# A later planned landing for the up stage's weight loads, the parts of T ahead of the first two GLU tiles, and two products of the down stage accumulated in banks that already hold a product

## The chip, the cores and the metric

One core of one Trainium2 chip runs the whole program. The metric is the device time of one execution in microseconds (us). The engines are TensorE (PE, with its weight loads as PEld), VectorE (DVE), ScalarE (ACT), GpSimd (POOL) and SyncE (SP); SP and POOL issue the transfers here.

## The reference

One decoder layer over 512 tokens with 1024 features, all in float32. The first half (projection, retention, sparse attention, output projection, norm) is not touched by the change. The second half is

```
def conv_ffn(x, w_up, conv_w, w_down):
    u = x @ w_up                                  # 512x1024 @ 1024x5632
    u = causal depthwise convolution of width 3 over the tokens
    gate, val = split(u, 2)
    return (gelu(gate) * val) @ w_down            # 512x2816 @ 2816x1024

h = rms_norm(x, norm_ffn_pre)
x = x + rms_norm(conv_ffn(h, ...), norm_ffn_post)
```

## The kernel before

Every float32 product is made of three fast products of a rounded high part and a low remainder (high by high, high by low, low by high), so each operand has to be split: ACT copies the high part, DVE subtracts it for the low part.

**The planner.** The code does not emit instructions as it goes. Every call on an engine is recorded as an operation, with a rank: a stage number and, within a stage, its place in the program. At the end `schedule` (L262) runs through the operations with a cost for each, and at each step gives an engine the operation that can start first; among those within 20 ns of it, the one of the lowest rank. Transfers get a modelled landing (L366 to L369): one transfer after the other at 350 bytes per ns (175 for accumulating ones), and then 2000 ns for SP and 4000 ns for POOL. What comes out is a fixed order of instructions for each engine; on the chip each engine works through its own list and waits where the next instruction's operands aren't there. The costs only shape this order. Two engines that touch the same PSUM bank are ordered one after the other even where both only read (L209, L214).

**The up stage** (L1247 to L1376) makes 22 pairs of tiles of gate and value, 128 columns each. The first two pairs are plain products, `up` (L1223), into four PSUM banks `ab` of the pool `acc`, which has four. Pairs 2 to 21 are made by a Strassen scheme (`strassen`, L1293): seven products of 12 matmuls each, P1, P2, P6, P5, P7, P3, P4 in this order, P1, P6, P7, P4 in a bank `X` of the pool `m` (three banks) and P2, P5, P3 in a bank `G` of `acc`. ACT copies interim sums out of the banks (`u` twice, `p5`) before the next product may add to them. The moving operands are the hidden states and sums of their quarters, the parts of T: `MV["5"]`, `MV["6"]`, `MV["7"]` and one more for `MV["4"]`, split at L1343 to L1351. For each pair `loads` (L1266) issues three transfers on SP (`a11`, `s1`, `a12`) and four on POOL, of which three add onto what an earlier transfer or a negated copy by ACT left there (`s1`, `s3`, `w["4"]`); `prep` (L1282) makes the six split weight tiles with ACT and DVE. `loads` of the next pair is recorded before `strassen` of this one. `glu` (L1238) takes a finished pair through convolution, gelu and product; `act_sums` (L1251) adds three sums for each two pairs. The order recorded around the change is: the plain products, `glu(0)`, `glu(1)`, the parts of T, `loads(2)`, `prep(2)`, `loads(3)`, Strassen pair 2 and its `glu`, and so on.

**The down stage** (L1431 to L1530) is also a Strassen scheme. P1, P5, P6, P7 are accumulated over all 11 pairs into eight banks `DA`; sums of them go to SBUF as `base` (L1444 to L1452). Then P4, P2, P3 run in banks of their own (`E`, L1454); `norm` (L1456) adds each finished product to its `base`, squares and sums on ACT, takes the root on POOL (`rsqrt`, a power), multiplies by the norm's weights (`wfin`), scales, adds the residual and sends it out. `norm(0)` and `norm(1)` are the last work of the program; the last three pairs of P2 and P3 are made bank by bank (`end`, L1522), so that the norms can follow.

Of the kernel before, what the change touches and what calls it, by code (L numbers as in the profile page):

```python
# [12 lines left out]
ALU = mybir.AluOpType  # L13
# [117 lines left out]
PE, ACT, DVE, POOL, SP = "tensor", "scalar", "vector", "gpsimd", "sync"  # L131
# [9 lines left out]


class _Op:
    __slots__ = ("idx", "alts", "rank", "deps", "nwait", "users", "news", "tiles", "start", "end", "eng", "ready", "gelu", "floor", "load", "port")


class _Plan:


    def __init__(self, nc):  # L150
        self.nc, self.ops, self.slots, self.hist, self.order_of = nc, [], {}, {}, {}
        self.rank, self.floor = 0, None

    def engine(self, *names):
        plan = self
# [30 lines left out]
    def add(self, alts):  # L186
        op = _Op()
        method, a, k = next(iter(alts.values()))
        op.idx, op.rank = len(self.ops), (self.rank, len(self.ops))
        op.alts = {n: (*x, self.cost(n, *x)) for n, x in alts.items()}  # L190
        op.load = 0.0
        op.port = {n: self.shared(n, *x) for n, x in alts.items()}
        if PE in alts:
            op.load = size(a[1]) / (2.4 if method == "transpose" else 1.2)
        op.gelu = next((x for x in list(a) + list(k.values()) if x in (AF.Gelu_apprx_tanh, AF.Exp, AF.Tanh)), None)
        op.deps, op.users, op.news, op.tiles = {}, [], [], set()
        acc = [(x, i == 0 or n in OUTS) for i, (n, x) in enumerate([(str(i), x) for i, x in enumerate(a)] + list(k.items()))
               if isinstance(x, bass.AP)]
        for ap, w in acc:
            name = ap.tensor.name  # L200
            if name not in self.slots:
                continue
            op.tiles.add(name)
            if name not in self.hist:
                self.hist[name] = []
                op.news.append(name)
                self.order_of[name] = len(self.order_of)
            pm, fm = self.region(ap)
            psum = "PSUM" in str(ap.space)  # L209
            keep = []  # L210
            for e in self.hist[name]:
                j, w2, pm2, fm2 = e
                hit = pm & pm2 and fm & fm2
                if hit and j != op.idx and (w or w2 or psum and self.ops[j].alts.keys() != alts.keys()):  # L214
                    op.deps[j] = op.deps.get(j, False) or (w2 and not w)
                if not (w and hit and not (pm2 & ~pm) and not (fm2 & ~fm)):
                    keep.append(e)
            keep.append((op.idx, w, pm, fm))
            self.hist[name] = keep
        op.floor = self.floor if any(x[0] == "dma_start" for x in alts.values()) else None  # L220
        self.ops.append(op)
        return op
# [39 lines left out]
    def schedule(self):  # L262
# [52 lines left out]
        while len(order) < len(ops):  # L315
# [50 lines left out]
            if method == "dma_start":  # L366
                nbytes = a[0].size() * 4 if callable(a[0].size) else a[0].size * 4
                dma = max(dma, op.end) + nbytes / (175.0 if "accum_op" in k else 350.0)
                op.end = dma + (2000 if e == SP else 4000)  # L369
            for x in op.alts:  # L370
                avail[x].remove(op)
            for t in op.tiles - live:
# [30 lines left out]
def _body(ctx, tc, io, out, soff, coff):  # L403
# [50 lines left out]
    def mps(n="m"):  # L454
        return plan.tile(pp, [P, 512], F32, nm(n), "m", 3)
# [124 lines left out]
                          C("ks").unsqueeze(1).to_broadcast([P, 4, RH]), op=ALU.mult)  # L580


    def mm3(o, ah, al, bh, bl, start, stop):
        pe.matmul(o, ah, bh, start=start, stop=False)
        pe.matmul(o, ah, bl, start=False, stop=False)
        pe.matmul(o, al, bh, start=False, stop=stop)

    class Chunk:
        def __init__(self, src, lh, ll, ncols, evac, first=0):
# [648 lines left out]
    def glu(i, ag, av):  # L1238
        g = conv(ag, i)
        act.activation(g, g, AF.Gelu_apprx_tanh)  # L1240
        v = conv(av, NF + i)
        (dve_pool if i >= PL else dve).tensor_tensor(acts[i // 2][:, i % 2, :], g, v, op=ALU.mult)
        if i % 2:
            act_sums(i // 2)
# [21 lines left out]
    def loads(i):  # L1266
        g, v = io["wup"][i, 0], io["wup"][i, 1]
        a, s13 = blk(gp, "av", 4, F32), blk(st, "raw", 2, F32)
        w = {"4": blk(gp, "av", 4)}
        a11, a12, s1, s3 = a[:, 0], a[:, 1], s13[:, 0], s13[:, 1]  # L1270
        sync.dma_start(a11, g[:, 0:4])
        sync.dma_start(s1, v[:, 0:4])
        sync.dma_start(a12, g[:, 4:8])
        pool.dma_start(s1, v[:, 4:8], accum_op=ALU.add)
        copy(s3, a11, scale=-1.0)
        pool.dma_start(s3, v[:, 0:4], accum_op=ALU.add)
        pool.dma_start(w["4"][:, 1], v[:, 4:8])
        copy(w["4"][:, 0], f(w["4"][:, 1]), scale=-1.0)
        pool.dma_start(w["4"][:, 0], v[:, 4:8], accum_op=ALU.add)
        return a11, a12, s1, s3, w  # L1280

    def prep(a11, a12, s1, s3, w):  # L1282
        s24 = blk(st, "wl", 4, F32)
        b2, b4 = s24[:, 0], s24[:, 1]
        dve.tensor_tensor(b2, s1, a11, op=ALU.subtract)
        for n, src, tag in (("1", a11, "wh"), ("2", a12, "wh"), ("6", b2, "wh"), ("5", s1, "wh"), ("7", s3, "wl"), ("3", b4, "wl")):
            if n == "6":
                dve.tensor_tensor(b4, a12, b2, op=ALU.subtract)
            w[n] = blk(st, tag, 4)
            part(w[n], src)  # L1290
        return w
# [34 lines left out]
    for c0 in (0, 256):  # L1326
        for i in range(4):
            up(ab[i], ws[i], c0, c0 + 256)
    glu(0, ab[0], ab[1])
    glu(1, ab[2], ab[3])  # L1330
    MV = {n: (h2h[q][:, :, c:c + HT], h2l[q][:, :, c:c + HT]) for n, q, c in (("1", 0, 0), ("2", 1, 0), ("3", 1, HT))}
    for a in range(2):
        k = slice(2 * a, 2 * a + 2)
# [7 lines left out]
    MV["7"] = None, t3l  # L1341
    MV["4"] = h2h[0][:, :, HT:], h2l[0][:, :, HT:]
    for n, src in (("5", [t13[0]]), ("6", hb[0]), ("7", [t13[1]]), ("4", hb[1])):  # L1343
        if n == "7":
            MV[n] = vv([P, 4, HT], F32R, "T"), t3l
        h, l = MV[n]
        w = 4 // len(src)
        for a, x in enumerate(src):
            k = slice(a * w, a * w + w)
            copy(h[:, k], x)  # L1350
            dve.tensor_tensor(l[:, k], x, f(h[:, k]), op=ALU.subtract)  # L1351
# [12 lines left out]
    def v_parts(j):  # L1364
        v = part2(pt, [P, 2, HT], "a")
        split(sm_s[j], *v)
        return v

    nxt = loads(PL)
    for i in range(PL, NF):  # L1370
        now = prep(*nxt)
        if i + 1 < NF:
            nxt = loads(i + 1)
        else:
            uv = u_parts(0), v_parts(0)
        glu(i, *strassen(i, now))  # L1376
# [23 lines left out]
    def wtile(n):  # L1400
        return tuple(plan.tile(st, [P, 2, 512], F32R, nm(m), m, 4) for m in ("wh", "wl"))

    def product(o, a, b, tt, start, stop):
        (ah, al), (bh, bl) = a, b
        ts = slice(tt * P, tt * P + P)
        mm3(o, ah[:, ts], al[:, ts], bh, bl, start, stop)

    def wrow(j, odd):
        return io["wdn"][2 * j + odd].rearrange("p a (b c) -> p (a b) c", b=2)
# [34 lines left out]
    for tt in range(2):  # L1444
        b = k8([P, 4, 512], n="base")
        x1, u3, u4, c22 = (b[:, q] for q in range(4))
        copy(x1, DA["1"][tt])
        dve.tensor_tensor(u4, DA["6"][tt], x1, op=ALU.add)
        dve.tensor_tensor(u3, DA["7"][tt], u4, op=ALU.add)
        dve.tensor_tensor(c22, DA["5"][tt], u3, op=ALU.add)  # L1450
        dve.tensor_tensor(u4, DA["5"][tt], u4, op=ALU.add)
        base[tt], base[2 + tt] = (x1, u4), (u3, c22)  # L1452

    E = {n: [t("d") for _ in range(2)] for n, t in (("4", mps), ("2", acc), ("3", acc))}  # L1454

    def norm(t, parts, o=None):  # L1456
        o = o or base[t]
# [45 lines left out]
    for j in range(NP):  # L1503
        wo = rawtile() if j < NP - TAIL else late[j - NP + TAIL]
        sync.dma_start(wo, wrow(j, 1))
        dve.tensor_tensor(sm_s[j][:, 1], acts[j][:, 1, 0:HT], sm_s[j][:, 1], op=ALU.subtract)
        z = wtile("z") if j < NP - TAIL else part2(s4, [P, 2, 512], "z")
        split(wo, *z)
        a12, a4 = pt([P, 2, HT], F32R, "a"), pt([P, 2, HT], F32R, "a")
        split(acts[j][:, 1, 0:HT], a12[:, 0], a12[:, 1])  # L1510
        split(sm_s[j][:, 1], a4[:, 0], a4[:, 1])
        jobs = {n: ((a[:, 0], a[:, 1]), [q[:, i] for q in z]) for n, a, i in (("2", a12, 0), ("3", a4, 1))}
        ends.append(jobs)
        if j < NP - TAIL:
            for n in "23":
                for tt in range(2):
                    product(E[n][tt], *jobs[n], tt, j == 0, False)
        if j == 0:
            for tt in range(2):
                norm(2 + tt, (E["4"][tt], None))  # L1520

    def end(n, tt):  # L1522
        for j in range(NP - TAIL, NP):
            product(E[n][tt], *ends[j][n], tt, False, j == NP - 1)

    for tt in range(2):
        end("2", tt)
        end("3", tt)
        norm(tt, (E["2"][tt], E["3"][tt]), [outs[:, tt, c] for c in range(2)])
    plan.emit(tc)  # L1530


# [12 lines left out]
```

## Time and profile before

| | us |
|---|---|
| median of 3 runs | 639.9 (639.33 to 641.75) |
| the profiled execution's own time | 637.82 |
| its span, first to last instruction | 635.9 |
| PE busy in the span | 614.5 |
| DVE busy in the span | 548.7 |
| ACT busy in the span | 430.6 |

The profile comes from one execution. A helper at L398 emits every operation, so its rows all show that line; the names of the tiles tell them apart: `b` are the weight tiles of the up stage, `G` and `X` its banks, `wup` its weights in memory, `d` the banks of the down stage, `o` its output.

### The profile page before, as it was taken

The page shows a single profiled execution, that of the slowest core. Times are in us where ns is not written, and L with a number is a line of the kernel's source. Part 1 is how long each engine was busy: PE and PEld are TensorE (multiplying, and loading weights), DVE is VectorE, ACT ScalarE, POOL GpSimd, SP SyncE. Part 2 cuts the span into 40 slices and gives each one's busy share as a digit, 9 for nine tenths or more (in the row PEclk, how much of TensorE's full clock was granted, in tenths as well). Part 3 has the DMA queues.
Part 4 walks back from the last instruction along what each step waited for, and adds up shares of the span by engine and source line. Part 5 has one row for each costly group of instructions (what it writes and reads, how often), then busy time and mean ns, then how long its engine had stood idle before and what let it go on. Part 6 is the DMA issues. An engine that isn't in the chain of part 4 may idle for free.

```text
span 635.9 us, 10876 instructions
## 1 busy us (share of the span) xinstructions
PE 614.5 (97%) x3781; PEld 543.4 (85%) x3781; DVE 548.7 (86%) x1163; ACT 430.6 (68%) x882; POOL 172.1 (27%) x205
## 2 busy tenths in 40 slices
PE   7999999999999989999999899999999999999995
PEld 4887998888878877879999899999999997887874
DVE  5369886898878899478999899999999999999995
ACT  5568566778997733465866667767677667777751
POOL 0064432543212415024032323233232212231000
PEclk9999899999999999999999999999999999999998
DMA  7762349522412332438358787887878558997452
GB/s 263 285 235 85 118 132 199 106 61 75 93 33 94 107 96 104 163 135 216 84 130 186 172 178 173 208 176 190 186 181 197 118 167 186 244 269 226 166 182 83
DMA packets 41527, 100.21 MB, mean 158 GB/s; under 512 B 4736, under 2 KB 4864, under 8 KB 41472
## 3 DMA queue, kind: packets, MB, share of 16 engines
q0 software_dynamic: 17424, 36.97, 30.4%
q1 hardware_dynamic: 23904, 62.29, 28.1%
q8 instruction: 30, 0.49, 0.3%
q10 hardware_dynamic: 144, 0.26, 0.1%
q14 instruction: 25, 0.20, 0.1%
HBM read 95.30 MB, written 4.19 MB: 156 GB/s over the span
## 4 chain that ended last, share of the span: by engine, by line
PE 61%; DVE 15%; issue 8%; DMA 8%; ACT 5%; POOL 2%; SPq 0%; DVEq 0%; POOLq 0%; ACTq 0%
PE acc L398 17%; PE X L398 15%; PE G L398 11%; DMA b<-wup 4%; PE tp L398 4%; PE pv L398 3%; PE wo L398 3%; PE s L398 3%; DVE wl L398 3%; PE cacc L398 2%; PE d L398 2%; POOL T L398 2%; ACT wh L398 1%; DMA T<-wdn 1%; DVE Tc L398 1%
## 5 line engine op out<-in xcount | busy, mean ns | idle before, releaser
L398 ACT ACTIVATE b<-b 128x512 fp32r<-128x512 f32 (+1 forms) x160 | 95.4, 624 | 21.0 <-DMA b<-wup 8.8
L398 DVE TENSOR_TENSOR b<-b,b 128x512 fp32r<-128x512 f32 (+1 forms) x160 | 106.3, 689 | 3.8 <-ACT b L398 2.5
L398 POOL DMA_DIRECT2D b<-wup x80 | 63.5, 918 | 150.7 <-ACT b L398 69.0
L398 PE MATMUL acc<-wl,xh 128*128 128x512 f32 (+1 forms) x192 | 74.8, 389 | 1.0 <-DVE wl L398 1.0
L398 PE MATMUL acc<-wh,xh 128*128 128x512 f32 (+1 forms) x192 | 73.7, 389 | 1.5 <-DVE wh L398 1.5
L398 PE MATMUL acc<-wh,xl 128*128 128x512 f32 (+1 forms) x192 | 73.9, 385 | 0.0
L398 ACT ACTIVATE wh<-raw 128x1024 fp32r<-128x1024 f32 (+2 forms) x51 | 51.9, 1018 | 32.0 <-PE acc L398 9.4
L398 DVE TENSOR_TENSOR wl<-raw,wh 128x1024 fp32r<-128x1024 f32 (+2 forms) x52 | 61.7, 1195 | 6.9 <-ACT wh L398 6.6
L398 PE MATMUL G<-h2h,b 128*128 128x256 f32 x320 | 64.6, 284 | 2.1 <-ACT p L398 2.1
L398 PE MATMUL X<-T,b 128*128 128x256 f32 x480 | 64.7, 284 | 1.5 <-ACT u L398 1.5
L398 PEld LDWEIGHTS X<-T,b 128*128 128x128 f32 x480 | 60.4, 192 | 2.4 <-ACT u L398 2.3
L398 PE MATMUL X<-h2h,b 128*128 128x256 f32 x320 | 61.1, 283 | 0.0
L398 PEld LDWEIGHTS G<-h2h,b 128*128 128x128 f32 x320 | 52.8, 192 | 2.7 <-ACT p L398 2.7
L398 PEld LDWEIGHTS X<-h2h,b 128*128 128x128 f32 x320 | 51.4, 192 | 0.1
L398 PE MATMUL X<-h2l,b 128*128 128x256 f32 x160 | 45.3, 283 | 0.0
L398 PE MATMUL G<-h2l,b 128*128 128x256 f32 x160 | 45.3, 283 | 0.0
L398 PEld LDWEIGHTS acc<-wh,xh 128*128 128x128 f32 x192 | 36.9, 194 | 7.8 <-issue 2.3
L398 PEld LDWEIGHTS acc<-wl,xh 128*128 128x128 f32 x192 | 37.2, 194 | 7.0 <-DVE wl L398 1.7
L398 PEld LDWEIGHTS acc<-wh,xl 128*128 128x128 f32 x192 | 37.2, 194 | 5.5
L398 ACT ACTIVATE P<-P,nmx 128x256 f32<-128x256 f32 (+3 forms) x64 | 35.2, 553 | 4.7 <-DVE nmx L398 4.6
L398 PE MATMUL d<-wl,ah 128*128 128x512 f32 x88 | 34.2, 393 | 0.9 <-DVE wl L398 0.9
L398 POOL DMA_DIRECT2D T<-wdn x21 | 18.2, 880 | 60.6 <-ACT T L398 43.9
(288 smaller groups left out, 1652.0 us busy)
## 6 DMA issues: line engine op xcount, KB each, us to landing
b<-wup POOLq DMA_DIRECT2D x80, 256.0 KB, 4.9
b<-wup SPq DMA_DIRECT2D x60, 256.0 KB, 4.0
raw<-wdn SPq DMA_DIRECT2D x19, 512.0 KB, 5.0
T<-wdn POOLq DMA_DIRECT2D x21, 256.0 KB, 6.0
raw<-wo SPq DMA_DIRECT2D x8, 512.0 KB, 3.2
T<-wdn SPq DMA_DIRECT2D x10, 256.0 KB, 5.6
xraw<-xT SPq DMA_DIRECT2D x8, 256.0 KB, 6.3
xnat<-x SPq DMA_DIRECT2D x4, 512.0 KB, 6.6
```

The source lines that it names most:

```text
L398: i = getattr(getattr(self.nc, op.eng), method)(*a, **k)
```

## The change

In the planner an operation gets a further number, `late`, that is added to the modelled landing of a transfer. `loads` is recorded with 800 ns for it; other transfers keep 0. In the up stage `glu(0)` is recorded after the parts 5, 6 and 7 of T and ahead of that for P4, and `glu(1)` after `prep(2)`. In the down stage P2 and P3 get no banks of their own: P2 goes on in the banks of P1, and P3 in those of P5, to which DVE first adds the sum that stood in `base`. The two norms of these tiles then read the banks themselves, with no addition.

```
@@ schedule
-                op.end = dma + (2000 if e == SP else 4000)
+                op.end = dma + (2000 if e == SP else 4000) + op.late
@@ up stage
-    glu(0, ab[0], ab[1])
-    glu(1, ab[2], ab[3])
     for n, src in (("5", [t13[0]]), ("6", hb[0]), ("7", [t13[1]]), ("4", hb[1])):
+        if n == "4":
+            glu(0, ab[0], ab[1])
...
+    LATE = 800
+    plan.late = LATE
     nxt = loads(PL)
+    plan.late = 0
     for i in range(PL, NF):
         now = prep(*nxt)
+        if i == PL:
+            glu(1, ab[2], ab[3])
         if i + 1 < NF:
+            plan.late = LATE
             nxt = loads(i + 1)
+            plan.late = 0
@@ down stage
-        dve.tensor_tensor(u4, DA["5"][tt], u4, op=ALU.add)
-        base[tt], base[2 + tt] = (x1, u4), (u3, c22)
-
-    E = {n: [t("d") for _ in range(2)] for n, t in (("4", mps), ("2", acc), ("3", acc))}
+        dve.tensor_tensor(DA["5"][tt], DA["5"][tt], u4, op=ALU.add)
+        base[tt], base[2 + tt] = (DA["1"][tt], DA["5"][tt]), (u3, c22)
+
+    E = {"4": [mps("d") for _ in range(2)], "2": DA["1"], "3": DA["5"]}
...
-                    product(E[n][tt], *jobs[n], tt, j == 0, False)
+                    product(E[n][tt], *jobs[n], tt, False, False, skip_group_check=True)
...
-            product(E[n][tt], *ends[j][n], tt, False, j == NP - 1)
+            product(E[n][tt], *ends[j][n], tt, False, j == NP - 1, skip_group_check=True)
...
-        norm(tt, (E["2"][tt], E["3"][tt]), [outs[:, tt, c] for c in range(2)])
+        norm(tt, (None, None), [outs[:, tt, c] for c in range(2)])
```

## Rows read from the trace of the kernel before

**Rows 1.** The page: its span, and busy time, share and instructions by engine.

```profile
span 635.9 us, 10876 instructions
PE 614.5 (97%) x3781; PEld 543.4 (85%) x3781; DVE 548.7 (86%) x1163; ACT 430.6 (68%) x882; POOL 172.1 (27%) x205
```

**Rows 2.** Windows: busy us (instructions) of PE, PEld, DVE, ACT, POOL; clock; DMA; GB/s.

```profile
310.00:320.00 10.00, 9.48 (x77) 9.06 (x76) 10.00 (x16) 8.21 (x15) 0.00 (x0) 1.00 0.30 75
...
360.00:370.00 10.00, 8.47 (x71) 8.26 (x70) 8.01 (x16) 6.27 (x12) 3.16 (x4) 1.00 0.84 196
...
380.00:390.00 10.00, 9.24 (x77) 9.04 (x76) 9.39 (x18) 6.84 (x14) 3.18 (x4) 1.00 0.90 216
...
450.00:500.00 50.00, 50.00 (x419) 50.00 (x419) 47.90 (x82) 35.90 (x70) 15.75 (x20) 1.00 0.80 184
```

**Rows 3.** PE's timeline, 352 to 386: start, us, what, idle before and its releaser.

```profile
352.55 0.39 PE L398 MATMUL G<-h2h,b 128*128 128x256 f32 x1 [0.27 <-ACT p L398]
...
361.29 1.60 PE L398 MATMUL X<-T,b 128*128 128x256 f32 x12
364.42 0.38 PE L398 MATMUL G<-h2h,b 128*128 128x256 f32 x1 [1.53 <-ACT p L398]
...
373.72 1.69 PE L398 MATMUL X<-T,b 128*128 128x256 f32 x12 [0.17 <-ACT u L398]
...
384.56 1.69 PE L398 MATMUL X<-T,b 128*128 128x256 f32 x12 [0.76 <-ACT u L398]
```

**Rows 4.** ACT's timeline ahead of the second and the fourth of these stops.

```profile
362.46 0.63 ACT L398 ACTIVATE b<-b 128x512 f32<-128x512 f32 x1 [0.83 <-DMA b<-wup]
363.46 0.63 ACT L398 ACTIVATE b<-b 128x512 fp32r<-128x512 f32 x1 [0.37 <-DMA b<-wup]
364.00 0.37 ACT L398 ACTIVATE p<-G 128x256 f32<-128x256 f32 x1
...
383.09 1.15 ACT L398 ACTIVATE b<-b 128x512 f32<-128x512 f32 x2 [0.85 <-DMA b<-wup]
```

**Rows 5.** Waits of ACT from 345 to 390: us in total, times, longest.

```profile
ACT b L398 <- DMA b<-wup: 4.0, 6, 1.0
```

**Rows 6.** The page's DMA issues: queue, count, KB each, median us to landing.

```profile
b<-wup POOLq DMA_DIRECT2D x80, 256.0 KB, 4.9
b<-wup SPq DMA_DIRECT2D x60, 256.0 KB, 4.0
```

**Rows 7.** PE's timeline in the first Strassen pair.

```profile
316.94 1.69 PE L398 MATMUL X<-T,b 128*128 128x256 f32 x12 [0.52 <-ACT u L398]
...
322.28 0.38 PE L398 MATMUL G<-h2h,b 128*128 128x256 f32 x1 [0.26 <-ACT p L398]
```

**Rows 8.** DVE's timeline there: the first and the last work of the second GLU tile.

```profile
311.69 0.75 DVE L398 SCALAR_TENSOR_TENSOR v<-up,sm,v 128x511 f32<-128x511 f32 x1
...
317.79 0.69 DVE L398 TENSOR_TENSOR act<-v,v 128x512 f32<-128x512 f32 x1
```

**Rows 9.** The end, all engines' timelines: PE's last matmul, and what follows it.

```profile
628.21 0.39 PE L398 MATMUL d<-zh,a 128*128 128x512 f32 x1
...
629.13 0.68 DVE L398 TENSOR_TENSOR base<-d,base 128x512 f32<-128x512 f32 x1
629.85 0.69 DVE L398 TENSOR_TENSOR o<-base,wfin 128x512 f32<-128x512 f32 x1
...
629.91 0.63 ACT L398 ACTIVATE junk<-base 128x512 bf16<-128x512 f32 x1 [1.80 <-DVE base L398]
...
630.66 0.16 DVE L398 SCALAR_TENSOR_TENSOR fs<-fs 128x1 f32<-128x1 f32 x1
631.48 1.41 DVE L398 SCALAR_TENSOR_TENSOR o<-o,fs,x 128x512 f32<-128x512 f32 x2 [0.66 <-POOL fs L398]
```

**Rows 10.** Timelines near 282: the same two steps on operands in a PSUM bank.

```profile
281.49 0.60 ACT L398 ACTIVATE junk<-wo 128x512 bf16<-128x512 f32 x1 [0.16 <-PE wo L398]
...
282.29 0.69 DVE L398 TENSOR_TENSOR mix<-wo,wpost 128x512 f32<-128x512 f32 x1
```

More of the change, by code (lines that the diff above doesn't have):

```diff
@@ L143 @@
 class _Op:
-    __slots__ = ("idx", "alts", "rank", "deps", "nwait", "users", "news", "tiles", "start", "end", "eng", "ready", "gelu", "floor", "load", "port")
+    __slots__ = ("idx", "alts", "rank", "deps", "nwait", "users", "news", "tiles", "start", "end", "eng", "ready", "gelu", "floor", "load", "port", "late")
 class _Plan:
@@ L151, in __init__ @@
         self.nc, self.ops, self.slots, self.hist, self.order_of = nc, [], {}, {}, {}
-        self.rank, self.floor = 0, None
+        self.rank, self.floor, self.late = 0, None, 0
     def engine(self, *names):
@@ L190, in add @@
         op.alts = {n: (*x, self.cost(n, *x)) for n, x in alts.items()}
-        op.load = 0.0
+        op.load, op.late = 0.0, self.late
         op.port = {n: self.shared(n, *x) for n, x in alts.items()}
@@ L580, in input_norm, with mm3 @@
                           C("ks").unsqueeze(1).to_broadcast([P, 4, RH]), op=ALU.mult)
[L583 to L586, printed above, removed]
+    def mm3(o, ah, al, bh, bl, start, stop, **k):
+        pe.matmul(o, ah, bh, start=start, stop=False, **k)
+        pe.matmul(o, ah, bl, start=False, stop=False, **k)
+        pe.matmul(o, al, bh, start=False, stop=stop, **k)
     class Chunk:
@@ L1401, in wtile, with product @@
         return tuple(plan.tile(st, [P, 2, 512], F32R, nm(m), m, 4) for m in ("wh", "wl"))
-    def product(o, a, b, tt, start, stop):
+    def product(o, a, b, tt, start, stop, **k):
         (ah, al), (bh, bl) = a, b
         ts = slice(tt * P, tt * P + P)
-        mm3(o, ah[:, ts], al[:, ts], bh, bl, start, stop)
+        mm3(o, ah[:, ts], al[:, ts], bh, bl, start, stop, **k)
     def wrow(j, odd):
```

## The prediction

> **What bounds the kernel now.** The page comes first: PE is busy for 97% of the span [rows 1], so only two things can save time, PE's stops and what runs after its last matmul. The windows show where the stops are: from 450 to 500 us PE is busy for all 50 us and DVE for 47.90 of them [rows 2]. So the settled part of the up stage has nothing to give, and DVE is a close second bound there, with some 4% of slack: over a pass (84 matmuls, one every 0.12 us by the 419 in 50 us [rows 2], 10.1 us) that is 10.1 x 2.1 / 50 = 0.42 us. The windows at 360 and 380 are another matter: PE falls to 8.47 and 9.24 of 10, and DVE to 8.01 and 9.39 [rows 2]. When both wait, something else is late.
>
> PE's timeline names the four stops [rows 3]. What a stop costs is a little more than the idle time beside it. At 361.29 twelve matmuls begin, so the next is due at 361.29 + 12 x 0.12 = 362.73; it begins at 364.42, 1.69 us late, and refills for 0.1, while the row shows 1.53 idle: the cost is the idle time plus about 0.26. That makes 0.53, 1.79, 0.43 and 1.02, in all 3.8 us. Each was released by a copy on ACT, `p` or `u`, which only reads a bank that PE itself had filled. ACT's timeline shows why such copies are late: the copy `p` at 364.00 is queued behind weight copies that waited 0.83 and 0.37 us for a transfer, and the fourth stop has the same pattern, with a wait of 0.85 [rows 4]. From 345 to 390 ACT waited six times for weights, 4.0 us in all, 1.0 at most [rows 5]. So these stops are a matter of order on ACT: an urgent copy stands behind one whose operand lands later than the plan has it. The planner's SP landing is 2.0 us and 0.75 for 256 KB, 2.75 us; the rows show 4.0 at the median for SP and 4.9 for POOL [rows 6].
>
> The first Strassen pair has two stops, 0.52 and 0.26 idle, so 0.78 + 0.52 = 1.3 us [rows 7]. DVE is busy for all of the window at 310 [rows 2]; between the first and the last work of the second GLU tile stand the low parts of T and of the weights that this pair waits for [rows 8].
>
> At the end PE's last matmul ends at 628.21 + 0.39 = 628.60. Then come, one behind the other, the addition onto `base` (629.13), the square (629.91), the sum (630.66), the root on POOL, and the scaling at 631.48 [rows 9].
>
> **The change, part by part.**
>
> *Later landing.* 800 ns is added to the planned landing of all seven transfers of `loads`; no transfer is itself held back. What can change is order: SP's and POOL's lists have the same transfers, each released by the same readers, and on ACT and DVE the work that needs a load is planned 0.8 us later, so that a `u` or `p` copy that is ready goes ahead. Six waits of 4.0 us, each 0.8 shorter, would leave under 0.3. The upper bound is therefore all 3.8 us of the four stops. The lower bound is nothing, or below it: the negated copies of `a11` and of `w["4"]` release accumulating transfers on POOL, and each copy that is put back delays its landing and then `prep`. The settled windows, which have an order of the same kind and no stop, speak for the upper half; that SP's shortfall (4.0 against 2.75) is more than 0.8 speaks for a remainder. I take two thirds, -2.5 us.
>
> *Parts of T first, second GLU tile after `prep(2)`.* No instruction is added or removed, and none of what is moved issues a transfer. `glu(1)` is four convolution steps and a product on DVE, 4 x 0.75 + 0.69 = 3.7 us, that leave the queue ahead of `prep(2)`; between its first and its last work lie 318.48 - 311.69 = 6.8 us [rows 8], so some 3.1 us of that are parts of T and of weights. `glu(0)` is moved past the parts of T, at most about those 3.1 us, and it frees the bank for the first `G` after its first two steps; that bank is wanted 12 matmuls, 1.4 us, after PE enters the pair. On ACT the copies for T likewise go ahead of `glu`'s. So at most 1.3 us of stops go. But DVE is full here, and what is put back must be done before the fourth `G`, some two passes later, since `glu(1)` holds two of the four banks: PE, entering earlier, presses on a full DVE. The gain may only move. Bounds: -1.3 to +1.3 (a first `G` that comes late, by as much as both stops together; this is a guess at the size, from the nearest stops). I take half the gain, -0.6 us.
>
> *P2 and P3 in the banks of P1 and P5.* Four DVE additions go; the one that now writes to the bank of P5 replaces one that wrote to SBUF. Three of the four lie beside PE. The last is on the path: the square can begin at about 628.68 instead of 629.91, which is 1.23 us (0.53 of it DVE being busy with `o` of the half before, 0.60 the addition, 0.1 the handover). Reading from a bank is no dearer: the square took 0.60 there against 0.63, the product with the weights 0.69 in both places [rows 9, 10]. The product of the last half used to run beside the square, at 629.85 and 629.91 [rows 9]; both now read one bank, and the planner orders them. So it must come behind the square: under the root, between the sum at 630.66 and the scaling at 631.48, DVE idles 0.66 [rows 9], and it has 0.60 to place. It has the lower priority against the sum, so it should fit; if it goes ahead of the sum, 0.6 is lost again. Bounds -0.6 to -1.3, taken -1.2 us.
>
> The Trainium skill, "PSUM — Partial Sum Buffer", Terms, goes further than the planner: two engines on one bank and the same partitions at once are a collision, two reads included. By that rule the overlap of square and product cannot come back by another order, and the saving at the end would stay between 0.6 and 1.2 us; no row here shows two engines on one bank at once.
>
> For the first of the two norms the additions lie beside PE's last products, so nothing is gained there; if they did press on DVE, each would be worth 0.6. P2 begins behind P4 as before, long after the sums that it waits for.
>
> **The sum.** -2.5 - 0.6 - 1.2 = -4.3 us. Against the profiled execution's own 637.82 us that is 633.5; this execution lay 2.1 us under the median of the runs, 639.9. The same saving from the median gives 635.6 us, 0.7% less.
>
> **The rivals.**
>
> *Only the end is won.* The change of planned landing may leave ACT's order as it is where it matters, or the wait moves to the next thing: DVE, which is full at 310 and at 96% in the settled part. For it: DVE's 10.00 at 310 and 47.90 of 50 [rows 2]; a stop that goes at 317 can come back at 335. Against it: DVE was idle for 2.0 us at 360 when PE was [rows 2], so DVE wasn't the bound at the largest stop. This also covers that the 800 ns don't do what they say. Time: 639.9 - 1.2 = 638.7.
>
> *All is won.* All four stops, both first ones and the end: 3.8 + 1.3 + 1.2 = 6.3, so 633.6. For it: all four have one cause. Against it: DVE would then have to do in the same time what it does now with 2% to 4% of slack.
>
> *Slower: the loads' loop gets too long.* Place: ACT's negated copies, which release POOL's accumulating transfers. A pair's raw weights live in two sets of buffers, so landing (4.0), copy (0.6), accumulating transfer (0.9 to issue, 4.9 to land) and `prep` must fit into two passes, 20 us. If the planner, thinking all loads later, puts the copies behind other work on ACT in each pass, `prep` comes late in each, and DVE idles. It decides from the point where DVE idles more per pass than its slack of 0.42: at 0.7 us, each of some 18 passes is 0.3 us longer, +5.4, and with the end's -1.2 this gives 644.1. For it: DVE is so close to PE that a small wait in each pass shows. Against it: 4.0 + 0.6 + 5.8 = 10.4 us leaves half of the two passes free.
>
> **How the numbers follow.** The forecast, 635.6, with 0.47; only the end, 638.7, 0.30; all is won, 633.6, 0.14; slower, 644.1, 0.09. A difference of 0.5% (3.2 us) is about what a measurement of this kernel can tell from no change, so faster means under 636.7. That takes in all of the third case and most of the first, whose own range is 634.5 to 638: 0.14 + 0.40 = 0.54. Slower by over 0.5%, above 643.1, is most of the last case, 0.07. Within is the rest, 0.39. The range leaves out the slower case and the very best: 633.0 (6.3 us and somewhat more of DVE's order) to 640.2 (nothing won in the up stage, a first `G` late by 0.9, and 0.6 at the end).
>
> **What would show it.** Right: in the windows from 350 to 390 PE at 9.9 or more; ACT's waits for weights under 1 us in all; no row with `p` or `u` as releaser and over 0.3 idle; the square within 0.15 us of the end of PE's last matmul, and the scaling 1.7 us behind that end, where it is 2.9 now (631.48 - 628.60). Wrong: PE stops between 313 and 352, with DVE named as releaser, or a short idle time in each pass from 400 on; the product with `wfin` standing between square and sum. The prediction fails if the new order is another one altogether, since one moved operation can change the greedy choice of every later one.

## The result, and the profile after

The changed kernel takes 635.53 us in the median of its runs (632.27 to 638.35), the kernel before 638.96 beside it (633.52 to 644.21); the ratio is 0.995, with a 95% interval of 0.9932 to 0.9968. So 3.2 us are saved, between 2.0 and 4.3. The forecast was 635.6 and 0.7%. The time came out nearly as forecast, but the experiments below show that its parts did not.

The profiled execution of the changed kernel took 637.12 us, with a span of 635.2, only 0.7 less than the span of before. The table takes five stretches from PE's timeline: up to the first product of the up stage, from there to the last product into a bank `X` or `G`, to the first product of P4, to the end of PE's last matmul, and to the last instruction. The last row but one has the instruction order of before in its first three stretches.

| us | to the up stage | up stage | to P4 | P4 to PE's end | after PE |
|---|---|---|---|---|---|
| before | 287.67 | 232.86 | 61.83 | 46.24 | 7.30 |
| changed | 287.15 | 232.28 | 63.65 | 46.04 | 6.08 |
| e3_banks | 284.89 | 234.31 | 62.10 | 46.40 | 6.10 |
| f1_order_banks | 285.23 | 231.74 | 62.33 | 46.41 | 6.09 |

Two profiles of one order differ by 2.8 us in the first stretch and by 1.5 in the second (287.67 - 284.89, 234.31 - 232.86). Stops and waits differ as much. ACT's waits for up weights from 310 to 516 are 4.9 and 8.8 us in the two profiles of the order of before (the second is e3_banks), 5.7 and 2.2 in two of the changed kernel's order in the up stage (the second is e4_late_order, an experiment below), 2.6 and 5.7 in two of a third order (e2_order and f1_order_banks). SP's landings and the way to P4 repeat better: 4.0 and 4.5, 5.8 and 5.8, 3.9 and 4.1 us, and 61.83 and 62.10, 63.65 and 64.05, 61.95 and 62.33. So single profiles serve here for what waits on what, for landings and for the last two columns; the ratios come from many runs.

The page of the changed kernel, its first two rows (span; busy us, share and instructions), and its rows of DMA issues (queue, count, KB each, median us to landing), which answer [rows 1, 6]:

```profile
span 635.2 us, 10860 instructions
PE 613.9 (97%) x3781; PEld 542.4 (85%) x3781; DVE 547.1 (86%) x1159; ACT 430.0 (68%) x882; POOL 179.1 (28%) x205
...
b<-wup POOLq DMA_DIRECT2D x80, 256.0 KB, 5.9
b<-wup SPq DMA_DIRECT2D x60, 256.0 KB, 5.8
```

Four DVE instructions are gone, as the diff says. The landings are the surprise: they grew from 4.9 and 4.0 us [rows 6] to 5.9 and 5.8.

The windows of the changed kernel, columns as in [rows 2]:

```profile
310.00:320.00 10.00, 10.00 (x83) 9.80 (x82) 10.00 (x17) 9.17 (x18) 1.77 (x3) 1.00 0.48 113
...
360.00:370.00 10.00, 10.00 (x86) 10.00 (x85) 10.00 (x19) 7.26 (x15) 3.19 (x4) 1.00 0.73 147
...
380.00:390.00 10.00, 9.26 (x75) 8.86 (x75) 8.17 (x15) 5.68 (x12) 2.97 (x4) 1.00 0.98 211
...
450.00:500.00 50.00, 48.93 (x405) 48.53 (x405) 47.64 (x82) 34.87 (x68) 15.84 (x20) 1.00 0.76 170
```

PE's fall at 360 [rows 2] is gone, that at 380 is still there, and the window from 450 to 500, full in before, has lost 1.07 us. PE's timeline has the stops from 310 us to the end of the up stage, all of 0.17 us and more, against those in [rows 3, 7]:

```profile
327.41 1.45 PE L398 MATMUL X<-T,b 128*128 128x256 f32 x10 [0.43 <-DVE b L398]
...
388.48 0.39 PE L398 MATMUL G<-h2h,b 128*128 128x256 f32 x1 [0.57 <-ACT b L398]
389.15 1.46 PE L398 MATMUL X<-T,b 128*128 128x256 f32 x10 [0.17 <-DVE b L398]
...
495.11 0.39 PE L398 MATMUL G<-h2h,b 128*128 128x256 f32 x1 [1.06 <-ACT p L398]
```

With 0.26 for each, that is 2.23 + 4 x 0.26 = 3.3 us, where before had 3.8 + 1.3 = 5.1. ACT's timeline ahead of the last of them has the pattern of [rows 4] unchanged: the copy `p` stands behind a weight copy that waited for a transfer.

```profile
494.15 0.63 ACT L398 ACTIVATE b<-b 128x512 fp32r<-128x512 f32 x1 [0.83 <-DMA b<-wup]
494.69 0.37 ACT L398 ACTIVATE p<-G 128x256 f32<-128x256 f32 x1
```

ACT's waits for up weights are 5.7 us in all from 310 to 516, no less than the 4.9 us of before in that stretch. The new order reaches PE's list too. In the changed kernel, as in the five other kernels here in which `LATE` is not 0, the first Strassen product stands in the midst of the plain ones (behind 96 or 100 of 192), 14 to 16 us behind the first of them; where it is 0, behind all 192, 24.7 us or more:

```profile
301.24 0.28 PE L398 MATMUL X<-h2h,b 128*128 128x256 f32 x1
301.36 0.28 PE L398 MATMUL up<-h2l,wh 128*128 128x256 f32 x1
```

On the way to P4 the changed kernel has four stops with 2.40 us idle, before three with 1.08.

The end of the changed kernel, all engines' timelines, against [rows 9]:

```profile
628.73 0.39 PE L398 MATMUL d<-zh,a 128*128 128x512 f32 x1
...
629.21 0.60 ACT L398 ACTIVATE junk<-d 128x512 bf16<-128x512 f32 x1 [1.35 <-PE d L398]
...
629.93 0.16 DVE L398 SCALAR_TENSOR_TENSOR fs<-fs 128x1 f32<-128x1 f32 x1 [1.25 <-ACT junk L398]
630.01 0.68 DVE L398 TENSOR_TENSOR o<-d,wfin 128x512 f32<-128x512 f32 x1
...
630.75 1.42 DVE L398 SCALAR_TENSOR_TENSOR o<-o,fs,x 128x512 f32<-128x512 f32 x2
```

PE ends at 629.12, the square begins 0.09 later, the sum goes ahead of the product with the weights, and the product fits under the root: it ends at 630.69, and the scaling begins at 630.75, 1.63 us after PE's end, where it was 2.88.

### The profile page after: what moved, and what is told of

Its sections match the earlier page's. It is cut to its first block, busy times and chain, and to the rows that moved or that the text cites. A ratio compares the mean times of both kernels' runs of the same rounds, so it can differ in the third digit from the quotient of the medians.

```text
span 635.2 us, 10860 instructions
## 1 busy us (share of the span) xinstructions
PE 613.9 (97%) x3781; PEld 542.4 (85%) x3781; DVE 547.1 (86%) x1159; ACT 430.0 (68%) x882; POOL 179.1 (28%) x205
## 5 line engine op out<-in xcount | busy, mean ns | idle before, releaser
L398 DVE TENSOR_TENSOR b<-b,b 128x512 fp32r<-128x512 f32 (+1 forms) x160 | 103.8, 683 | 2.7 <-ACT b L398 1.5
L398 ACT ACTIVATE b<-b 128x512 fp32r<-128x512 f32 (+1 forms) x160 | 92.6, 624 | 15.1 <-DMA b<-wup 6.8
L398 PE MATMUL d<-wh,ah 128*128 128x512 f32 x88 | 33.1, 395 | 1.6 <-ACT wh L398 1.6
```

The lines of the kernel that those rows point to most:

```text
L398: i = getattr(getattr(self.nc, op.eng), method)(*a, **k)
```

## The experiments

Each ratio is against the kernel before, run beside it, with its 95% interval.

**One part at a time.** Three theories stood: that of the prediction (the later landing carries the saving), that only the end is won, and that the loads' loop gets too long.

```
e1_late: only the late number and LATE = 800 around loads(...)
```

> The kernel before with the 800 ns of planned landing alone. The theory of the prediction: -2.5 us of 638.96 (0 to -3.8), 636.5; PE's stops from 345 to 390 us, 3.8 us in the profile of before, fall under 1.5, and none of them is released by p or u behind a weight copy. The rival that only the end is won: 638.5 to 639.5, stops at other places of the same sum. The rival of the loads' loop: over 641, with idle time on DVE in each pass.

Measured: 0.9975 (0.9943 to 1.0007); 1.6 us saved, or nothing. The four stops from 345 to 395 are gone in its profile, but `u` and `p` copies still stop PE at 313 (1.16 idle), 400 (0.69) and 510 (0.80), and ACT waits 4.6 us for weights. SP's landing went up to 5.5 us by its page. The stops moved; the theory's -2.5 is inside the interval, and so is 0.

```
e2_order:  for n, src in (...):
+              if n == "4": glu(0, ab[0], ab[1])
           ...
           now = prep(*nxt)
+          if i == PL: glu(1, ab[2], ab[3])
```

> The kernel before with the parts of T ahead of the GLU of pair 0, and that of pair 1 behind the first preparation, alone. The theory of the prediction: -0.6 us (-1.3 to +1.3); the first pair's two stops, 1.3 us, go, and half comes back on a full DVE before 350. The rival that only the end is won: 0. The four stops from 345 to 390, which have another cause by the theory, stay, some 3 to 4 us in all.

Measured: 0.9932 (0.9902 to 0.9962), 4.4 us saved, seven times the forecast's term and beyond its bound. From 310 us on its profile has two stops in the up stage, 0.59 idle at 327 and 0.54 at 350. The four stops from 345 to 395, which the theory gave to another cause, went with the order; the one at 350 is at another place than they were.

```
e3_banks: only base, E, product(..., False, ...) and norm(tt, (None, None), ...)
```

> The kernel before with P2 and P3 accumulated in the banks of P1 and P5 alone; the order of the work up to the base sums is that of before. All theories: from PE's last matmul's end to the last instruction 6.1 us, where it is 7.3 in before, so -1.2 us (-0.6 to -1.3). The time: 637.8 of 638.96. If it were -3 the change's gain would be at the end alone.

Measured: 0.9948 (0.9917 to 0.9979); 3.3 us, 1.3 to 5.3. The time after PE is 6.10 us, as expected. What the ratio has beyond 1.2 has no place in the profile: its up stage ran in the order of before, and was not faster. Its stops there show how much one order varies from one execution to another:

```profile
313.45 1.70 PE L398 MATMUL X<-T,b 128*128 128x256 f32 x12 [0.53 <-ACT u L398]
...
318.68 0.39 PE L398 MATMUL G<-h2h,b 128*128 128x256 f32 x1 [0.17 <-ACT p L398]
...
359.70 0.39 PE L398 MATMUL G<-h2h,b 128*128 128x256 f32 x1 [0.41 <-ACT p L398]
...
381.02 1.70 PE L398 MATMUL X<-T,b 128*128 128x256 f32 x12 [2.35 <-ACT u L398]
...
420.05 1.69 PE L398 MATMUL X<-T,b 128*128 128x256 f32 x12 [1.33 <-ACT u L398]
```

These and one at 329 (0.25) are 5.04 us idle; in the profile of before, the same order had 3.51 [rows 3, 7], in part at the same places with other lengths (the stop 71.4 us behind the first Strassen product took 0.76 there and 2.35 here), in part at others. So 1.2 at the end is what is shown, and a larger effect of this part is neither shown nor excluded. The 2 us or so between the two are also a measure of what a ratio can hold that no profile explains.

```
e4_late_order: e1 and e2 together
```

> Both edits of the up stage, without the one of the down stage. The theory of the prediction: the two add up, -3.1 us, 635.9, and with the end's -1.2 the changed kernel. The rival that only the end is won: within 0.5 us of before, as the changed kernel's saving of 3.4 would then have to come from the end.

Measured: 0.993 (0.9899 to 0.9962), the ratio of the order alone. The parts don't add up: beside the order, the later landing brings nothing that these runs can tell.

**The planned landing, with the other two parts kept.**

```
f1_order_banks: LATE = 0        g2_early800: LATE = -800
f3_late1600:    LATE = 1600     f2_late_early: plan.late = LATE if i < 12 else 0
```

> The changed kernel with the planned landing put back (0 for 800 ns): the new order of the parts of T and the GLU tiles, and the shared banks. The theory of the prediction, by which the later landing carries the saving: -1.8 us of before, ratio 0.997. The theory formed from the first four runs, by which the order carries it and the later landing costs some 2 us between the up stage's end and P4: -5 us, ratio 0.992, the stretch from the last up product to the first P4 product at 62 us, not 64, and SP's median landing of the up weights back at 4.0 us from 5.8.

Measured: 0.9918 (0.9892 to 0.9945), 5.2 us saved; to P4 62.33 us, SP's landing at 4.1 us on its page. These are the second theory's numbers, and far from the first's 0.997. Its profile doesn't show fewer stops, though: 3.10 us idle from 310 on, ACT's waits 5.7 us. It has the lowest ratio of the kernels here that compute the layer; but its interval overlaps that of the changed kernel (0.9932 to 0.9968), and the two were not timed side by side, so that the later landing costs something at 800 is likely and not shown.

> The changed kernel with the 800 ns only for the loads of pairs 2 to 12, none for 13 to 21. If the down stage's 2 us come from the landing planned later at the join of the two stages: the stretch from the last up product to the first P4 product at 62 us, and some 1.5 to 2 us less than the changed kernel (ratio 0.992). If they come from where the first half of the stage leaves the plan: 64 us and the changed kernel's 0.995.

Measured: 0.9973 (0.9937 to 1.0008), and 63.36 us to P4. It speaks against the join: without later landings from pair 13 on, the stretch is nearly as long as in the changed kernel, and nothing is won back. But the stretch doesn't go with the later landing alone: e1_late, which has it, needs 62.28 us to P4, and g4_glu0 and g3_no_accum, without it, 63.49 and 64.23. What sets this stretch was not found.

> The changed kernel with 1600 ns for 800. The theory of the prediction, by which a longer planned landing takes ACT's waits away: the waits of ACT for the up weights (5.7 us in the changed kernel) halve, PE's stops from 310 to 516 under 1 us, 1 us less than the changed kernel. The theory that landings grow along with the plan: SP's median landing over 6 us, ACT's waits about the same, time within 1 us of the changed kernel. The rival of the loads' loop: PE's stops in each pass, over 640 us.

Measured: 1.0035 (1.0005 to 1.0065), slower than before. ACT waited 8.0 us for weights, PE's stops from 310 to 516 come to 6.3 us idle, the way to P4 to 66.6. A longer planned landing did not take the waits away. SP's landing was 5.4 us, no longer than at 800, so that guess falls too. The stops stand singly, not in each pass, so it is not the loop of the rival either.

> The changed kernel with the landing planned 800 ns earlier than in the kernel before, not later. The ratios so far are 0.9918 at 0, 0.995 at 800, 1.0035 at 1600. If a later planned landing is a loss by itself, by a poorer order: 0.990 to 0.992 here. If 0 is near the best, since ACT waits longer for weights once they are planned too early: 0.995 or more, with ACT's waits over 7 us.

Measured: 1.0041 (0.9996 to 1.0085). ACT waited fifteen times, 8.6 us in all. So with order and banks kept the ratio goes 1.0041, 0.9918, 0.995, 1.0035 for -800, 0, 800 and 1600 ns: 0 is near the best, and both far ends lose.

What the number does can be counted from the traces. Take POOL's 80 loads of up weights in fours and PE's first product of each pair, and average over the last eight pairs. In before a load is issued 13.4 us ahead of its pair and lands 8.6 us ahead; in the changed kernel it is 9.4 and 3.2, at 1600 ns 9.2 and 3.4, in e1_late 11.0 and 5.3; in f1_order_banks 13.3 and 8.3, at -800 ns 13.4 and 8.1. So a later planned landing does hold loads back. By the kernel's code the likely way is that what reads a raw tile is planned later, its buffer comes free later, and the next load waits for it; no run shows this step by itself. SP's landings go with what is in flight beside them. Of its 60 loads, those with fewer than one POOL load in flight beside them, on average over their own time, took 3.4 us in before (29 of them) and 3.0 in the changed kernel (12); those with two or more took 6.2 (10) and 7.0 (29). In the five kernels with later landings 22 to 29 loads are of the last kind, in the other eight with 140 transfers 6 to 21.

**The two halves of the order.**

```
f4_glu1: glu(0) left in place; after prep(2):  if i == PL: glu(1, ab[2], ab[3])
g4_glu0: if n == "4": glu(0, ab[0], ab[1]); glu(1, ab[2], ab[3])
```

> The kernel before with the second GLU tile behind the first preparation alone; that of pair 0 stays ahead of the parts of T. If the order's saving of 4 us comes from taking glu(1) and its sums (some 4 us of DVE) out of the way of the first preparation: -3 us, ratio 0.995, ACT's waits for weights from 310 to 516 near the 2.6 us of the run with both moves. If it comes from the parts of T going ahead of glu(0): within 1 us of before, and the first pair's stops as there.

Measured: 0.9937 (0.9906 to 0.9968), as with both halves. ACT's waits came to 6.5 us in its profile, not 2.6, so that part of the expectation failed. Nor does this profile show 4 us: from the first product of the up stage to the first of P4 it takes 294.64 us, where before has 294.69 and e3_banks, in the order of before, 296.41. PE's stops from the first Strassen product on come to 2.96 us idle; e2 and f1 have 1.13 and 3.10, before, e3 and g4_glu0 3.51, 5.04 and 4.83. So the profiles bear out the direction and about half of the saving, and the ratios alone the rest.

> The kernel before with both GLU tiles behind the parts 5, 6 and 7 of T, glu(1) right behind glu(0) and ahead of the first preparation. If the saving comes from the parts of T: 0.994. If it comes from glu(1) standing behind the first preparation, as the run with that alone (0.9937) says: within 0.3% of before.

Measured: 1.0029 (1.0005 to 1.0052), slower than before. So the parts of T ahead of the GLU tiles save nothing by themselves; the second GLU tile behind the first preparation does. What that moves is seen in the loads of pair 4. Here are PE's first Strassen product, SP's ninth load of up weights (the third of pair 4, which needs a raw buffer that the preparation of pair 2 has read; DVE's part of that preparation releases it), POOL's ninth (the first of pair 4) and a later row of POOL, in e3_banks (the order of before), f4_glu1 and g4_glu0:

```profile
309.64 0.28 PE L398 MATMUL X<-h2h,b 128*128 128x256 f32 x1
...
316.49 0.33 SPq L398 DMA_DIRECT2D b<-wup  x1
...
317.43 0.86 POOL L398 DMA_DIRECT2D b<-wup  x1 [12.25 <-ACT b L398]
...
327.73 3.20 POOL L398 DMA_DIRECT2D b<-wup  x4 [6.44 <-ACT b L398]
```

```profile
309.98 0.28 PE L398 MATMUL X<-h2h,b 128*128 128x256 f32 x1
...
312.55 0.33 SPq L398 DMA_DIRECT2D b<-wup  x1
...
315.06 1.74 POOL L398 DMA_DIRECT2D b<-wup  x2 [9.60 <-ACT b L398]
...
325.18 0.85 POOL L398 DMA_DIRECT2D b<-wup  x1 [4.04 <-ACT b L398]
```

```profile
309.14 0.28 PE L398 MATMUL X<-h2h,b 128*128 128x256 f32 x1
...
316.87 0.33 SPq L398 DMA_DIRECT2D b<-wup  x1
...
317.82 0.86 POOL L398 DMA_DIRECT2D b<-wup  x1 [13.09 <-ACT p L398]
...
328.70 3.20 POOL L398 DMA_DIRECT2D b<-wup  x4 [7.45 <-ACT p L398]
```

SP's load begins 6.9, 2.6 and 7.7 us behind PE's first Strassen product (before itself 6.9, e2 and f1 3.5), POOL's 7.8, 5.1 and 8.7 (before 7.9, e2 and f1 5.1). The rows of POOL after that begin at 18.1, 15.2 and 19.6 (before 17.7, e2 and f1 15.3). With `glu(1)` behind, the last load of pair 4 goes there by itself; in the other orders it is one of four in a row, behind two of pair 5. So with `glu(1)` behind, the loads of pair 4 start 2.7 to 4.4 us earlier than in before and e3; with the parts of T and both GLU tiles ahead of `prep(2)` they start up to 0.9 us later still, and the time follows. The lead doesn't last: over the last eight pairs POOL's loads are issued 13.2 to 13.4 us ahead of their pair in all six kernels. That the earlier start is the cause fits all six, but no run moved the transfers alone.

**Are the stops late transfers?**

```
g3_no_accum, in loads(i):
+ if i < 4:
      pool.dma_start(s1, ..., accum_op=ALU.add)     # the same for s3 and w["4"][:, 0]
```

> The kernel before, with the three accumulating transfers of each pair left out from pair 4 on (the sums of the weights are not made there, and 54 of 140 transfers of the up stage with them). If the stops of the up stage are transfers that land late: PE's stops from 345 to 516 near 0, from 2.7 (4.1 in a second profile of the same order), ratio 0.993, as with the new order. If they have another cause, DVE's load above all: stops as in before, ratio within 0.3% of 1.

Measured: 0.9889 (0.9847 to 0.9931). From 319 us to 516 there is no stop. Its windows, columns as in [rows 2]:

```profile
360.00:370.00 10.00, 10.00 (x86) 10.00 (x85) 9.68 (x17) 7.29 (x14) 0.53 (x1) 1.00 0.38 113
...
400.00:450.00 50.00, 50.00 (x419) 50.00 (x419) 47.72 (x82) 36.86 (x70) 2.64 (x5) 1.00 0.34 106
450.00:500.00 50.00, 50.00 (x419) 50.00 (x418) 48.12 (x84) 36.36 (x70) 2.11 (x4) 1.00 0.33 100
```

DVE's and ACT's work is all there, DVE at 48 of 50, and PE never waits; ACT does not wait once for up weights, and the transfers that are left land in 3.0 us. So the stops are not DVE's load. They hang on the accumulating transfers; but with these go their own landings, the waits of what reads them and GpSimd's time for issuing them, and the planner makes a somewhat different list, and these were not taken apart. The first pair's two stops, from before the cut, are still there. The run saves more (7.1 us) than the stops in one profile of before.

```
g1_neg_pool, from f1:
- copy(s3, a11, scale=-1.0)
+ pool.tensor_scalar(s3, a11, -1.0, None, op0=ALU.mult)     # and likewise for w["4"][:, 0]
```

> The new order and the shared banks without the later landing (ratio 0.9918 in the run before), and in addition the two negated copies of each pair, which wait for a transfer, are made by GpSimd ahead of its own accumulating transfer, no longer by ACT. If PE's stops in the up stage are copies on ACT that stand behind such waits: ACT's waits for the up weights fall from 5.7 us to under 3, PE's stops released by u or p from 345 to 516 (2.5 us) to under 1, and 1 to 2 us are won (0.990). If GpSimd's share in the loads is the tighter one: the accumulating transfers land later, DVE waits for weights, slower than 0.9918.

Measured: 1.039 (1.0344 to 1.0436), much slower. ACT's waits for weights fell to 1.4 us, as expected, but the copies cost more than they free. The groups by line and shape (busy us, mean ns of one, idle before and its releaser):

```profile
L398 DVE TENSOR_TENSOR b<-b,b 128x512 fp32r<-128x512 f32 x120 | 86.9, 751 | 1.4 <-ACT b L398 1.4
...
L398 POOL TENSOR_SCALAR b<-b 128x512 fp32r<-128x512 f32 x20 | 42.5, 2123 | 13.6 <-DMA b<-wup 13.6
L398 POOL TENSOR_SCALAR b<-b 128x512 f32<-128x512 f32 x20 | 35.8, 1792 | 30.7 <-DMA b<-wup 12.1 <-ACT u L398 10.1 <-ACT b L398 6.1
```

A copy takes GpSimd 1.8 to 2.1 us for ACT's 0.62, its wait for the transfer now holds up the transfers queued behind it, and the low parts that DVE makes take 751 ns on average, where the page of before has 689. The average hides two kinds: of all 160 low parts of both shapes, the 108 with no work of GpSimd's but transfers beside them took 686 ns, at most 694; of the 52 others 20 took over 720, the longest 1757. Most of PE's stops have DVE's weights as releaser, 4.2 us the longest. It says nothing on `u` and `p` beyond this.

## Why the prediction was right, and where it was not

*The time and its range.* 635.53 against 635.6, and a saving of 0.5% against 0.7%: the likeliest case, within the range. The sum was near because two wrong terms made up for each other, and that is luck.

*What bounds.* PE with its stops: g3_no_accum shows that these hang on the accumulating transfers and not on DVE's load; that it is their late landing is likely, by the rows of ACT ahead of the stops, and not taken apart. The step that took their sum for 3.8 us from one profile is weak: the same order has 2.73 us idle from 345 to 395 in one execution, and 2.76 plus 1.33 at 420 in another.

*Later landing, -2.5 us.* This step failed. Taken alone it gave 1.6 or nothing; beside the order, nothing that can be told; at 1600 ns it made the kernel slower than before. The error lies in "no transfer is itself held back" and in "six waits of 4.0 us, each 0.8 shorter": they hold issue and landing fixed while the plan moves. POOL's loads were issued 9.4 us ahead of their pair for 13.4 before, and landed 3.2 ahead for 8.6. In all five kernels with later landings SP's transfers landed in 5.3 us or more, in the others with 140 transfers in 4.6 or less; ACT's waits came out at 5.7 us for 4.9, which is within what two profiles of one order differ by. The lower bound of that step, nothing or below, with copies put back that release transfers, was the better guess. The longer landings come with more of POOL's loads in flight beside SP's; no run moved the issues alone to show that this is the cause.

*Parts of T first, second GLU tile later, -0.6 us.* The step failed in size and in place: -4.4 us alone, beyond the bound of -1.3. The first pair's stops went, as said (one of 0.59 at 327 came in their place). What was missed is that `glu(1)` stands not only ahead of the weights of one pair but ahead of the release of raw buffers and so of the loads of the next pairs. (It also left out the three sums that `glu(1)` brings along, 0.43 us of DVE each.) The text counted DVE's work and said that "none of what is moved issues a transfer"; that what is moved holds up the release of some was not followed up. And of the two moves only the second pays. That this earlier start makes up the whole 4.4 us is not shown.

*Shared banks, -1.2 us.* Right, step by step: 7.30 to 6.08 us, the square 0.09 us behind PE, the sum ahead of the product, the product under the root. By the order seen, the square's read of the bank is over before the product reads it, so the rule of the Trainium skill's "PSUM — Partial Sum Buffer", Terms, was not put to the test; no row here shows two engines on one bank at once.

*The rivals.* That only the end is won is refuted by e2_order and e4_late_order, which save 4.4 and 4.5 us without it. The slow rival, the loads' loop, did not come in the form told; but planning 800 ns further did end slower than before, by single stops and a longer way to P4. *What would show it:* PE at 9.9 from 350 to 390 failed at 380 (9.26), ACT's waits under 1 us failed (1.2 from 345 to 390 in one wait, 5.7 over the stage), "no row with `p` or `u`" over 0.3 failed at 495 (1.06), the marks at the end held. Of the signs of being wrong, one came: a stop with DVE as releaser between 313 and 352 (0.43 at 327). A stop in each pass from 400 on did not, but a single one at 495, in a window that was full. And the case of the last sentence, another order altogether, came in part, as PE's own list shows.

## What to carry to other kernels

Before an allowance for late transfers is put into a planner, ask what the new order does to the issues and the landings themselves, and try it on both sides of the value: here nothing that can be told was won at 800 ns, and at 1600, as at -800, the whole gain of the other two edits was lost. Work that stands ahead of a preparation on a full engine also stands ahead of every buffer which that preparation frees; follow it to the next loads, not only to the next product. And where one order gives stops at other places in each execution, one profile tells their kind, not their sum.

## What the runs showed of the hardware

All of these kernels but g3_no_accum move the same number of bytes. Yet the median landing of SP's 256 KB was 3.9 to 4.6 us in those without a later planned landing (4.0 and 4.5 in two profiles of one order) and 5.3 to 5.8 in the five with one; with the accumulating transfers left out it was 3.0. In one profile it ranges from 3.0 us on average beside fewer than one POOL load in flight to 7.0 beside two or more (the changed kernel). In g1_neg_pool, where GpSimd makes copies of 128x512 elements, DVE's low parts took 686 ns on average with no work of GpSimd's but transfers beside them, and up to 1757 ns with a copy beside them; GpSimd's own transfers were issued in 1043 ns on average, where the other kernels with all 80 have 878 to 979.
